# Weight sums made by adding transfers, and a second seven-product form in the first pair of groups two to four of an MLP

## The chip, the cores and the metric

The kernel runs on one core of a Trainium2 chip. The metric is device time in microseconds (us) of one execution, the median of several runs. The engines are named as in the profile: PE (TensorE, matmuls) with PEld (its weight loads), DVE (VectorE), ACT (ScalarE), POOL (GpSimd) and SP (SyncE, which here only issues DMAs).

## What is computed

One decoder block on 256 tokens and 16 prepended meta tokens, with a model width of 2048, in float32:

```python
h = h + hybrid_mixer(rmsnorm(h, norm_mix_g[l]), ...)
h = h + squared_relu_mlp(rmsnorm(h, norm_mlp_g[l]), w_ff1[l], w_ff2[l])
return rmsnorm(h, final_norm_g)[:, N_META:]

def squared_relu_mlp(xn, w1, w2):
    return jnp.square(jax.nn.relu(xn @ w1)) @ w2
```

The mixer (forgetting attention beside gated linear attention) ends in two gates, two projections and an output projection w_out. The MLP has 8192 hidden columns; the mixer's outputs for the meta tokens aren't needed after it, so that the MLP works on 256 tokens.

## The kernel before

**Numbers.** Every float32 operand is split into a high part (a rounded copy, made by ACT) and a low part (the rest, subtracted by DVE), and a product of two operands is three matmuls: high x high, high x low, low x high. `cut` (L969) makes the split of a fetched tile of weights into a buffer `w`, of which there are five. The fetched tile itself, `raw`, has five buffers too.

**Pairs.** The MLP runs in four groups of 2048 hidden columns. In a group, the first MLP product (x2 times w_ff1, into `a`) takes two pairs, and the second (`a` times w_ff2) takes two more (in the last group one, whose columns 1024 on are done in another way by the tail). A pair (`pair_of`, L999) makes 1024 output columns, as two blocks f of 512, for 256 tokens, as two halves t of 128. Its contraction over 2048 rows goes in 16 row tiles of 128. The columns stage of the mixer, which makes the gates of 12 of the 16 column blocks, has three pairs of the same kind.

**Forms.** Two row tiles, both halves of the tokens and both blocks of columns make a plain step (`plain`): one fetched tile of weights (512 KB, 2 row tiles x 512 columns) per block, one split, and two products, one for each half of the tokens. A product (`product_into`, L987) is 2 x 3 = 6 matmuls of 128x512. Four row tiles at a time can instead be taken in a seven-product form: the operands are 2 x 2 blocks (two halves of the tokens by two pairs of row tiles; two pairs of row tiles by two blocks of columns), and 7 products (m1 to m7) of sums of blocks stand for 8. The sums of token blocks (`token_sums`, four of them, made by DVE and split) are kept in `s_x2` and `s_a`; the sums of weight blocks r11, r12, r21, r22 are made by DVE (`less`, L976, a subtraction of 128x1024) in held tiles hb, hc, hd, he (he is the tile sums4, which the profile calls sums). `pair_of` is given one or two token sums and then takes four or eight row tiles in one or two forms. Before, the second pair of the second MLP product in groups one to three, and the three pairs of the columns stage, have two forms; all others have one.

**What each step of a form does before.** `held` fetches r12 to b and r22 to c. `m1` fetches r11, multiplies it, and subtracts it from b. `m5` splits that difference and makes two more sums (with two forms) or one. `m6` and `m7` multiply the sums, `m3` multiplies r22 (fetched once more where there are two forms), `m2` fetches r21 and makes the last sum, and `m4` multiplies that. `m1` to `m7` add into four PSUM banks x, y, z, v, with two copies and two additions between them.

**Order.** The forms of the next pair are put between the plain steps of the present one: after plain step i run the form's steps n for which `at[n] == i` (a table of numbers in the main loop of the MLP, another in `columns`). A scheduler then sets each engine's order by priority. In the output projection before the MLP (a loop over 16 blocks j), the first pair's form is put after j = 3, 5, 8 and 11. Weight fetches are issued by SP, in order, as far ahead as there are free buffers; the reloads of s_x2 from its copy in DRAM (`kept_sums`, four quarters, at the start of the fourth pair's plain steps) are issued by POOL (L1378).

## Time and profile before

| | us |
|---|---|
| median of 3 runs | 1497.2 (1497.01 to 1497.43) |
| the profiled execution | 1497.08 |
| its span, first to last instruction | 1495.1 |
| PE busy | 1484.9 |
| DVE busy | 1193.2 |
| ACT busy | 878.4 |
| POOL busy | 119.8 |

The page divides the span into 40 equal slices and gives for each the busy share of an engine in tenths (9 is 90% or more), the clock that PE was granted and the busy share of the DMA engines. The chain that ended last is followed back from the last instruction, at each step to what released it. A row of a group of instructions has the line, engine and operation, what it writes and reads, shapes, the count, then busy us and mean ns of one, and then the idle time of the engine just before them and what ended it. In the kernel, DMAs moved 335.00 MB. The columns stage lies about at 480 to 690 us, the output projection at 755 to 840, the MLP at 840 to 1460.

### The profile page before, as it was taken

What the parts mean: (1) busy time and instruction counts of PE and PEld (TensorE: products, weight loads), DVE (VectorE), ACT (ScalarE), POOL (GpSimd) and SP (SyncE); (2) the same over time, 40 slices, a digit from 0 to 9 for tenths busy, and PEclk for the clock granted to TensorE, in tenths of its full rate; (3) what the DMA queues carried; (4) which work ended last, traced back from release to release, by engine and by line L of the source; (5) the groups of instructions that cost most, each with busy time, mean ns of one, the idle gap of its engine ahead of it and who ended that gap; (6) DMA issues with size and microseconds to landing.
All of it is one profiled execution on the core that took longest, in us unless ns stands there. A gap on an engine that the chain in (4) does not pass through costs nothing.

```text
span 1495.1 us, 22541 instructions
## 1 busy us (share of the span) xinstructions
PE 1484.9 (99%) x8374; PEld 1322.2 (88%) x8374; DVE 1193.2 (80%) x1578; ACT 878.4 (59%) x1246; POOL 119.8 (8%) x202
## 2 busy tenths in 40 slices
PE   9999999999999999999999999999999999999997
PEld 8999999999999888888988888888888888888887
DVE  7899858586677877876788889877998889898766
ACT  7765444455555555555566666666665566556645
POOL 6012100111111000000011100000000000000004
PEclk9999999999999999999999999999999999999999
DMA  9545555465547677678678678877777778888783
GB/s 325 176 145 185 182 170 180 159 213 170 169 163 247 212 224 233 205 230 286 223 248 253 204 248 264 267 230 242 250 244 249 230 250 252 266 260 273 249 277 110
DMA packets 242545, 335.00 MB, mean 224 GB/s; under 512 B 13130, under 2 KB 209748, under 8 KB 242180
## 3 DMA queue, kind: packets, MB, share of 16 engines
q1 hardware_dynamic: 219940, 299.22, 61.2%
q10 hardware_dynamic: 21360, 30.09, 6.5%
q0 software_dynamic: 1136, 4.27, 0.9%
q8 instruction: 65, 1.06, 0.3%
q14 instruction: 44, 0.36, 0.1%
HBM read 316.22 MB, written 17.31 MB: 223 GB/s over the span
## 4 chain that ended last, share of the span: by engine, by line
PE 96%; DVE 2%; issue 1%; ACT 1%; POOL 0%; POOLq 0%; DVEq 0%; ACTq 0%
PE bx L993 17%; PE ps L169 14%; PE bv L993 11%; PE by L993 11%; PE bz L993 11%; PE ps L170 7%; PE psa L174 5%; PE psa L178 5%; PE psa L176 4%; PE gla L993 4%; PE fox L993 2%; PE ps L429 1%; PE ps L431 1%; PE ps L1424 1%; DVE w L135 1%
## 5 line engine op out<-in xcount | busy, mean ns | idle before, releaser
L973 DVE TENSOR_TENSOR w<-raw,w 128x1024 fp32r<-128x1024 f32 x300 | 365.4, 1224 | 100.9 <-ACT w L972 96.6
L972 ACT CAST w<-raw 128x1024 fp32r<-128x1024 f32 x300 | 312.3, 1048 | 203.6 <-PE bx L993 68.2
L135 DVE TENSOR_TENSOR w<-raw,w 128x1024 fp32r<-128x1024 f32 x198 | 243.0, 1229 | 81.5 <-ACT w L134 80.1
L134 ACT CAST w<-raw 128x1024 fp32r<-128x1024 f32 x198 | 207.4, 1049 | 92.4 <-PE psa L178 30.3
L169 PE MATMUL ps<-x,w 128*128 128x512 f32 x543 | 184.4, 383 | 0.0
L174 PE MATMUL psa<-x,w 128*128 128x272 f32 x640 | 181.7, 285 | 0.0
L178 PE MATMUL psa<-x,w 128*128 128x272 f32 x640 | 179.6, 282 | 0.0
L176 PE MATMUL psa<-x,w 128*128 128x272 f32 x624 | 175.9, 282 | 0.0
L170 PE MATMUL ps<-x,w 128*128 128x256 f32 x543 | 149.0, 274 | 0.0
L993 PE MATMUL bx<-w,x 128*128 128x512 f32 x528 | 131.1, 381 | 0.0
L174 PEld LDWEIGHTS psa<-x,w 128*128 128x128 f32 x640 | 120.2, 188 | 0.2
L178 PEld LDWEIGHTS psa<-x,w 128*128 128x128 f32 x640 | 120.2, 188 | 0.1
L176 PEld LDWEIGHTS psa<-x,w 128*128 128x128 f32 x624 | 117.4, 188 | 0.0
L169 PEld LDWEIGHTS ps<-x,w 128*128 128x128 f32 x543 | 101.9, 188 | 17.1
L993 PEld LDWEIGHTS bx<-w,x 128*128 128x128 f32 x528 | 98.8, 188 | 17.4
L993 PE MATMUL by<-w,x 128*128 128x512 f32 x444 | 112.5, 381 | 0.0
L170 PEld LDWEIGHTS ps<-x,w 128*128 128x128 f32 x543 | 102.0, 188 | 0.0
L993 PEld LDWEIGHTS by<-w,x 128*128 128x128 f32 x444 | 83.2, 188 | 14.6
L993 PE MATMUL bv<-w,x 128*128 128x512 f32 x360 | 91.9, 381 | 0.0
L993 PE MATMUL bz<-w,x 128*128 128x512 f32 x360 | 91.6, 381 | 0.0
L169 PE MATMUL ps<-y,w 128*128 128x512 f32 x256 | 85.6, 380 | 0.0
L993 PE MATMUL bx<-w,a 128*128 128x512 f32 x336 | 83.7, 380 | 0.0
(405 smaller groups left out, 2741.1 us busy)
## 6 DMA issues: line engine op xcount, KB each, us to landing
raw<-w_all_dram SPq DMA_DIRECT2D x489, 512.0 KB, 4.6
there<-turn ACTq DMA_DIRECT2D x80, 128.0 KB, 3.9
turn<-there ACTq DMA_DIRECT2D x20, 512.0 KB, 4.7
hb<-w_all_dram SPq DMA_DIRECT2D x18, 512.0 KB, 4.4
hc<-w_all_dram SPq DMA_DIRECT2D x18, 512.0 KB, 5.3
raw<-w_all_dram SPq DMA_DIRECT2D x26, 256.0 KB, 5.0
raw<-w_all_dram SPq DMA_DIRECT2D x8, 384.0 KB, 6.8
hd<-w_all_dram SPq DMA_DIRECT2D x6, 512.0 KB, 7.1
```

The source lines that it names most:

```text
L134: copied = nc.scalar.copy(hi[:, k, :], r).ins
L135: return copied, nc.vector.tensor_tensor(lo[:, k, :], r, hi[:, k, :].bitcast(F32), op=ALU.subtract).ins
L169: nc.tensor.matmul(steps(ps), hi, steps(row(x)), start=first, stop=False)
L170: nc.tensor.matmul(steps(ps[:, 0:NT]), lo, steps(x[:, 0, :]), start=False, stop=last)
L174: nc.tensor.matmul(steps(ps[:, X_LO]), hi, steps(x_lo[:, k]), start=first, stop=False, skip_group_check=True)
L176: nc.tensor.matmul(steps(ps[:, 0:NA]), lo, steps(x_hi[:, k]), start=False, stop=last and hi is None, skip_group_check=True)
L178: nc.tensor.matmul(steps(ps[:, 0:NA]), hi, steps(x_hi[:, k]), start=False, stop=last, skip_group_check=True)
L429: nc.tensor.matmul(steps(ps), hi, steps(row(x[:, k])), start=st, stop=False)
L431: nc.tensor.matmul(steps(ps[:, 0:NT]), lo, steps(x[:, k, 0]), start=False, stop=sp)
L972: copied = nc.scalar.copy(hi, r).ins
L973: made(copied, nc.vector.tensor_tensor(lo, r, hi.bitcast(F32), op=ALU.subtract).ins, 1)
L993: nc.tensor.matmul(steps(ps), l, steps(r), start=start and k == 0 and i == 0, stop=False, skip_group_check=True)
```

## The change

A transfer issued by POOL adds r22, as it comes from DRAM, onto a held tile (`gain_block`, a DMA with an accumulating add): onto b after m1 has used it, and, with two forms, onto a after m5's split. The signs of the sums change with that, in `token_sums` too. r22 isn't fetched to a held tile of its own any more where there are two forms, and `less` is left with m1 and m2 (and m5, as an addition, with one form). a is now always a held tile, not the fetched r11.

With the tiles so freed, the first pair of the first MLP product in groups two to four takes two forms, with the sums of x2's first eight row tiles in s_x2 and s_a. The second sums are made in the output projection from blocks 4 to 7 (at j = 9), stored to DRAM at j = 13, and reloaded with the first in groups two to four. The tables of places change: in `columns` for the first pair, and in the MLP for the pairs with two forms and for those beside a shorter rest.

```diff
@@ token_sums
-        nc.vector.tensor_tensor(c, src(0, 1), src(1, 1), op=ALU.add)
-        nc.vector.tensor_tensor(s3, src(0, 0), src(0, 1), op=ALU.subtract)
-        nc.vector.tensor_tensor(d, c, src(0, 0), op=ALU.subtract)
+        nc.vector.tensor_tensor(c, src(0, 1), src(1, 1), op=ALU.subtract)
+        nc.vector.tensor_tensor(s3, src(0, 1), src(0, 0), op=ALU.subtract)
+        nc.vector.tensor_tensor(d, src(0, 0), c, op=ALU.subtract)
@@ columns
+    def gain_block(raw, c0, k0):
+        nc.gpsimd.dma_start(raw.rearrange("p (c k m) -> p c k m", k=2, m=P),
+                            w_all[c0 : c0 + 4, :, k0 * P : (k0 + 2) * P].rearrange("c p (k m) -> p c k m", m=P),
+                            accum_op=ALU.add)
@@ pair_of
         def held(q):
-            got["b", q], got["c", q] = fetched(f2, 4 * q, ("hb", "hd")[q]), fetched(f2, 4 * q + 2, ("hc", "he")[q])
+            got["b", q] = fetched(f2, 4 * q, ("hb", "hc")[q])
+            if nq == 1:
+                got["c", q] = fetched(f2, 4 * q + 2, "hc")
 
         def m1(q):
             r11 = fetched(f1, 4 * q)
             w = split_of(r11)
-            got["a", q] = r11 if nq > 1 else holder("hd")
+            got["a", q] = holder(("hd", "he")[q])
             less(got["a", q], got["b", q], r11)
+            gain_block(got["b", q], f2, 4 * q + 2)
             product("x", own(0, 4 * q), w, q == 0)
...
         def m5(q):
             w = split_of(got["a", q])
             if nq > 1:
-                less(got["b", q], got["c", q], got["b", q])
-                less(got["c", q], got["c", q], got["a", q])
+                gain_block(got["a", q], f2, 4 * q + 2)
             else:
-                less(got["a", q], got["c", q], got["a", q])
+                less(got["a", q], got["c", q], got["a", q], ALU.add)
             product("v", summed(q, 0), w, q == 0)
...
         def m6(q):
-            w = split_of(got["c" if nq > 1 else "a", q])
-            if nq == 1:
-                less(got["b", q], got["c", q], got["b", q])
+            w = split_of(got["a", q])
             product("x", summed(q, 1), w)
@@ pairs
-                yield (g, p), lambda: pair_of(blocks(), x2, [s_x2], lambda f, pt, g=g, p=p: hidden(
+                yield (g, p), lambda: pair_of(blocks(), x2, [s_x2, s_a] if p == 0 and g in TWO else [s_x2], lambda f, pt, g=g, p=p: hidden(
@@ output projection
-        if j < 4:
-            nc.vector.tensor_scalar(gained[:, NT * j : NT * (j + 1)], ht[:, j, :], gain(1, j), None, op0=ALU.mult)
-        if j == 3:
+        if j == 4:
+            gained = turn_tile()
+        if j < 8:
+            nc.vector.tensor_scalar(gained[:, NT * (j % 4) : NT * (j % 4 + 1)], ht[:, j, :], gain(1, j), None, op0=ALU.mult)
+        if j in (3, 9):
...
-            token_sums(s_x2, lambda i, t: g4[:, 2 * i : 2 * i + 2, t], gained[:, 4 * NT :])
+            token_sums(s_x2 if j == 3 else s_a, lambda i, t: g4[:, 2 * i : 2 * i + 2, t], gained[:, 4 * NT :])
...
-        if j == 8:
-            nc.scalar.dma_start(kept_sums, s_x2.bitcast(F32))
+        if j in (8, 13):
+            nc.scalar.dma_start(kept_sums[j // 13], (s_x2 if j == 8 else s_a).bitcast(F32))
@@ main loop of the MLP
-              3: (0, 2, 4, 5, 5, 6, 6, 7)}.get(index % 4, (0, 2, 3, 4, 5, 7, 9, 10))
+              3: (0, 1, 1, 3, 2, 3, 4, 4, 5, 5, 5, 6, 6, 6, 7, 7) if len(steps_next) > 8 else (0, 2, 4, 5, 5, 6, 6, 7),
...
-                    nc.gpsimd.dma_start(s_x2[:, q].bitcast(F32), kept_sums[:, q])
+                    for tile_of, kept_of in list(zip((s_x2, s_a), kept_sums))[0 : len(steps_next) // 8]:
+                        nc.gpsimd.dma_start(tile_of[:, q].bitcast(F32), kept_of[:, q])
```

How this moves instructions is shown at the first pair of group two, whose form or forms stand between the plain steps of the pair before it (the second pair of group one's second product). First PE, before: by, bx, bz, bv with the operand a are plain products, those with x2 or s_x2 belong to the form (m1 with w_1348, m5 with w_1356, m6 with w_1361).

```order
L993 MATMUL by_1307_9622<-w_1346_9912,a_1220_8986 128x4x32x4 x6
L993 MATMUL bx_1295_9529<-w_1346_9912,a_1220_8986 128x4x32x4 x6
L993 MATMUL bx_1350_9934<-w_1348_9929,x2_1064_7876 128x4x32x4 x6
L993 MATMUL by_1307_9622<-w_1353_9945,a_1220_8986 128x4x32x4 x6
L993 MATMUL bx_1295_9529<-w_1353_9945,a_1220_8986 128x4x32x4 x6
L993 MATMUL bz_1316_9690<-w_1355_9964,a_1220_8986 128x4x32x4 x6
L993 MATMUL bv_1300_9565<-w_1355_9964,a_1220_8986 128x4x32x4 x6
L993 MATMUL bv_1357_9983<-w_1356_9979,s_x2_7880 128x4x32x4 x6
L993 MATMUL bz_1316_9690<-w_1360_9994,a_1220_8986 128x4x32x4 x6
L993 MATMUL bv_1300_9565<-w_1360_9994,a_1220_8986 128x4x32x4 x6
L993 MATMUL bx_1350_9934<-w_1361_10009,s_x2_7880 128x4x32x4 x6
```

The same place on PE now, from the second form's m1 (w_1353) on; m5 has w_1357 and w_1359, m6 has w_1363 and w_1364.

```order
L999 MATMUL bx_1349_9927<-w_1353_9953,x2_1064_7870 128x4x32x4 x6
L999 MATMUL by_1306_9611<-w_1356_9968,a_1221_8993 128x4x32x4 x6
L999 MATMUL bx_1297_9538<-w_1356_9968,a_1221_8993 128x4x32x4 x6
L999 MATMUL bz_1319_9712<-w_1362_10010,a_1221_8993 128x4x32x4
L999 MATMUL bv_1301_9570<-w_1362_10010,a_1221_8993 128x4x32x4
L999 MATMUL bv_1358_9989<-w_1357_9985,s_x2_7874 128x4x32x4 x6
L999 MATMUL bv_1358_9989<-w_1359_9996,s_a_7875 128x4x32x4 x6
L999 MATMUL bz_1319_9712<-w_1362_10010,a_1221_8993 128x4x32x4 x5
L999 MATMUL bv_1301_9570<-w_1362_10010,a_1221_8993 128x4x32x4 x5
L999 MATMUL bx_1349_9927<-w_1363_10025,s_x2_7874 128x4x32x4 x6
L999 MATMUL bx_1349_9927<-w_1364_10034,s_a_7875 128x4x32x4
```

Between the start of m5 and that of m6 there stood 18 matmuls before; now there are 22, m5 of the second form among them.

DVE at the same place, before, from the split of m1's weights (w_1348) to that of m6's (w_1361): three subtractions (L977) make the sums, two of them behind m5's split.

```order
L973 TENSOR_TENSOR w_1348_9929<-raw_1347_9927,w_1348_9929 128x1024
L977 TENSOR_TENSOR hd_1349_9932<-hb_1341_9889,raw_1347_9927 128x1024
L973 TENSOR_TENSOR w_1353_9945<-raw_1352_9943,w_1353_9945 128x1024
L973 TENSOR_TENSOR w_1355_9964<-raw_1354_9962,w_1355_9964 128x1024
L973 TENSOR_TENSOR w_1356_9979<-hd_1349_9932,w_1356_9979 128x1024
L977 TENSOR_TENSOR hd_1349_9932<-hc_1342_9891,hd_1349_9932 128x1024
L973 TENSOR_TENSOR w_1360_9994<-raw_1359_9992,w_1360_9994 128x1024
L973 TENSOR_TENSOR w_1361_10009<-hd_1349_9932,w_1361_10009 128x1024
L977 TENSOR_TENSOR hb_1341_9889<-hc_1342_9891,hb_1341_9889 128x1024
```

DVE there now, from the last plain split ahead of the forms (w_1344) to that of the second m6 (w_1364). ACT's copies of the same tiles stand in the same order.

```order
L974 TENSOR_TENSOR w_1344_9902<-raw_1343_9900,w_1344_9902 128x1024
L974 TENSOR_TENSOR w_1347_9921<-raw_1346_9919,w_1347_9921 128x1024
L978 TENSOR_TENSOR hd_1348_9924<-hb_1342_9898,raw_1346_9919 128x1024
L974 TENSOR_TENSOR w_1351_9936<-raw_1350_9934,w_1351_9936 128x1024
L974 TENSOR_TENSOR w_1353_9953<-raw_1352_9951,w_1353_9953 128x1024
L978 TENSOR_TENSOR sums4_78<-hc_1345_9917,raw_1352_9951 128x1024
L974 TENSOR_TENSOR w_1356_9968<-raw_1355_9966,w_1356_9968 128x1024
L974 TENSOR_TENSOR w_1357_9985<-hd_1348_9924,w_1357_9985 128x1024
L974 TENSOR_TENSOR w_1359_9996<-sums4_78,w_1359_9996 128x1024
L974 TENSOR_TENSOR w_1362_10010<-raw_1361_10008,w_1362_10010 128x1024
L974 TENSOR_TENSOR w_1363_10025<-hd_1348_9924,w_1363_10025 128x1024
L974 TENSOR_TENSOR w_1364_10034<-sums4_78,w_1364_10034 128x1024
```

The subtractions between m5's and m6's splits are gone; in their place, hd and sums4 are added to by POOL's transfers, which no row of DVE shows. With five buffers, w_1357 takes the one of w_1344 (w_1347, w_1351, w_1353 and w_1356 lie between), and w_1359 that of w_1347.

POOL before had, between the sums of squares of the output projection and those of the tail, nothing but the reloads.

```order
L1207 TENSOR_TENSOR acc2_7885<-acc2_7885,hsq_1178_8702 128x256
L1207 TENSOR_TENSOR acc2_7885<-acc2_7885,hsq_1185_8754 128x256
L1207 TENSOR_TENSOR acc2_7885<-acc2_7885,hsq_1192_8806 128x256
L1378 DMA s_x2_7880<-kept_sums_7884 128x512 x12
L1207 TENSOR_TENSOR acc3_8813<-acc3_8813,hsq_1859_13611 128x256
```

POOL now, from the second form of the pair before (sums4_78) to the four additions of the first pair of group two (hb and hc after m1, hd and sums4 after m5):

```order
L981 DMA sums4_78<-w_all_dram 128x4x256
L1389 DMA s_x2_7874<-kept_sums_7878 128x512
L1389 DMA s_a_7875<-kept_sums2_7879 128x512
L1389 DMA s_x2_7874<-kept_sums_7878 128x512
L1389 DMA s_a_7875<-kept_sums2_7879 128x512
L1389 DMA s_x2_7874<-kept_sums_7878 128x512
L1389 DMA s_a_7875<-kept_sums2_7879 128x512
L981 DMA hb_1342_9898<-w_all_dram 128x4x256
L1389 DMA s_x2_7874<-kept_sums_7878 128x512
L981 DMA hc_1345_9917<-w_all_dram 128x4x256
L981 DMA hd_1348_9924<-w_all_dram 128x4x256
L981 DMA sums4_78<-w_all_dram 128x4x256
```

The reloads now alternate between s_x2 and s_a, and the additions stand among them in one queue: hc, hd and sums4 follow the last reload, with nothing between them.

More of the change, by code (lines that the diff above doesn't have):

```diff
@@ L1078, in m4 @@
         def m4(q):
-            product("x", own(1, 4 * q + 2), split_of(got["c" if nq > 1 else "a", q]))
+            product("x", own(1, 4 * q + 2), split_of(got["a", q]))
         if nq == 1:
```

15 lines of the change are left out of this document (9 added, 6 removed).

## The prediction, before the changed kernel ran

> **What bounds the kernel now.** I read the page first, then the waits of TensorE (PE), then the busy time by stretches, then the timeline at the place that the change makes tighter, and last the DMA issues. The page gives the span, the busy time, the 40 slices and the chain that ended last:
>
> ```profile
> span 1495.1 us, 22541 instructions
> PE 1484.9 (99%) x8374; PEld 1322.2 (88%) x8374; DVE 1193.2 (80%) x1578; ACT 878.4 (59%) x1246; POOL 119.8 (8%) x202
> PE   9999999999999999999999999999999999999997
> DVE  7899858586677877876788889877998889898766
> PEclk9999999999999999999999999999999999999999
> DMA  9545555465547677678678678877777778888783
> PE 96%; DVE 2%; issue 1%; ACT 1%; POOL 0%; POOLq 0%; DVEq 0%; ACTq 0%
> ```
>
> PE is busy in every slice at full clock and makes 96% of the chain. PE's own waits, longest first (us in total, times, longest), come to two us over the whole span:
>
> ```profile
> PE warm L393 <- DVE ones L274: 1.3, 1, 1.3
> PE pr L287 <- DVE csl L255: 0.3, 1, 0.3
> ```
>
> So a matmul that goes shortens the run by its own spacing, and nothing that DVE, ACT or DMA saves is worth anything, unless PE starts to wait. The price of a matmul is in the stretch of the MLP where only products run (us, then busy time and count of each engine, PE clock, DMA share, GB/s); the other rows are used below:
>
> ```profile
> 776.00:812.00 36.00, 36.00 (x210) 32.26 (x209) 33.24 (x41) 24.23 (x37) 6.35 (x6) 1.00 0.77 248
> 855.00:1425.00 570.00, 570.00 (x2593) 486.36 (x2592) 486.50 (x491) 360.33 (x413) 6.52 (x12) 1.00 0.79 251
> 1320.00:1340.00 20.00, 20.00 (x93) 17.06 (x92) 18.32 (x20) 11.00 (x12) 0.00 (x0) 1.00 1.01 325
> ```
>
> 570.00 / 2593 = 0.220 us for one 128x512 matmul. (A matmul's own 0.38 us overlaps its neighbours and is not its price.)
>
> **Part 1, fewer products.** A pair has 16 row tiles. With one seven-product form (four row tiles) it takes 7 products and 12 plain row tiles of 2 products each, 31 in all. With two forms it takes 14 and 8 x 2 = 16, so 30. Groups two to four have one such pair each: 3 products, of 6 matmuls each, 18 matmuls x 0.220 = 3.96 us. The built programs agree: 3744 matmuls of that line before, 3726 now. This is all on the path. It also excludes that the change doesn't do what it says.
>
> **Part 2, DVE and ACT.** One subtraction of 128x1024, one split on each engine, and the small steps of the sums cost:
>
> ```profile
> L973 DVE TENSOR_TENSOR w<-raw,w 128x1024 fp32r<-128x1024 f32 x300 | 365.4, 1224 | 100.9 <-ACT w L972 96.6 <-DMA turn<-there 1.2
> L972 ACT CAST w<-raw 128x1024 fp32r<-128x1024 f32 x300 | 312.3, 1048 | 203.6 <-PE bx L993 68.2 <-PE bv L993 61.6 <-issue 13.2
> L977 DVE TENSOR_TENSOR hb<-hc,hb 128x1024 f32<-128x1024 f32 x18 | 22.5, 1248 | 0.0
> L1267 DVE TENSOR_SCALAR turn<-h 128x256 f32<-128x256 f32 x4 | 2.8, 709 | 0.0
> L909 DVE TENSOR_TENSOR turn<-turn 128x256 f32<-128x256 f32 x1 | 0.4, 425 | 0.0
> L255 DVE TENSOR_TENSOR s_x<-turn,s_x 128x1024 fp32r<-128x1024 f32 x1 | 1.2, 1218 | 0.0
> ```
>
> Weight sums on DVE: before, 24 forms x 4 = 96; now 18 forms in two-form pairs x 2 and 9 alone x 3 = 63. That is 33 x 1.22 = 40 us less. Splits: a second form takes 7 where 4 plain row tiles took 4, so 9 more, 9 x 1.22 = 11 us on DVE and 9 x 1.05 = 9.4 us on ACT. None of it is on the path, so I cost both signs at nothing. The cover is the lead of the weights over PE, and it is thinnest in the output projection, where the second sums of x2 come in: 4 x 0.71 + 4 x 0.42 + 1.22 = 5.7 us more on DVE between j = 4 and 10, less 1.25 for the sum into hb that a transfer now makes. In the stretch 776 to 812 DVE has 33.24 of 36 us; with 4.5 more it is 1.7 us over. The lead must absorb that; below I say what if not.
>
> **Part 3, the transfers.** SP issues 12 fetches fewer (a form's own stay at four, and the three new second forms replace four plain fetches each), POOL issues 45 adding transfers of 512 KB (18 x 2 + 9), and 24 reloads of 256 KB instead of 12; ACT stores a second 1 MB of sums once. That is 33 x 0.524 + 12 x 0.262 + 1.05 = 21.5 MB on top of 335.0, spread over stretches where the DMA engines stand at 0.79. Each adding transfer must also read the 512 KB that it adds to. I cost this at nothing except in one stage.
>
> **Part 4, the new wait.** An adding transfer makes ACT's split wait for a landing where it used to wait for a DVE subtraction. Behind that split in ACT's queue stand all later splits and the copies out of PSUM; behind a transfer in POOL's queue stand the reloads of the sums and the next transfers; SP's fetch into hb waits for the split of m7, as before. How far apart are the product that starts the transfer (m5: its split releases a) and the product that needs it (m6)? By the new order of PE at 0.220 us per matmul, start to start: 7.9 to 14.5 us in the column pairs, 10.6 and 11.9 us in the second pair of the second product. But in the first pair of groups two to four m5 starts at 8.36 us after the last product of w_1344 and m6 at 13.20: 38 and 60 matmuls later, 4.84 us apart. For m7 it is 14 us or more. So only this place is tight, three times.
>
> The time allowed is that distance, plus the lead with which m5's split is done before PE uses it, less one split on ACT and DVE. The same place in before, m5 and m6 of group two's first pair, shows the lead:
>
> ```profile
> 979.40 1.23 DVE L973 TENSOR_TENSOR w<-hd,w 128x1024 fp32r<-128x1024 f32 x1 [1.30 <-ACT w L972]
> 987.32 1.48 PE L993 MATMUL bv<-w,s_x 128*128 128x512 f32 x6
> 983.80 1.22 DVE L973 TENSOR_TENSOR w<-hd,w 128x1024 fp32r<-128x1024 f32 x1 [0.53 <-ACT w L972]
> 991.28 1.48 PE L993 MATMUL bx<-w,s_x 128*128 128x512 f32 x6
> 942.50 1.23 DVE L973 TENSOR_TENSOR w<-sums,w 128x1024 fp32r<-128x1024 f32 x1
> 945.52 0.38 PE L993 MATMUL bx<-w,s_x 128*128 128x512 f32 x1
> ```
>
> The first two pairs of rows give 987.32 - 980.63 = 6.7 us and 991.28 - 985.02 = 6.3 us. The last pair, 40 us earlier, where DVE also has four subtractions, gives 1.8 us. In the new order five weight buffers set the lead: w_1357 (m5) takes that of w_1344, free at 0; 1.05 + 1.22 = 2.3 us later it is split, 6.1 us ahead of PE. I take 6.1, since DVE has only 22 splits and 4 subtractions (32 us) in this stage's 30 x 6 x 0.220 = 39.6 us. Allowed: 4.84 + 6.1 - 2.3 = 8.6 us, and for the second form 8.6 too, since both its products stand one product later.
>
> What does an adding transfer take? No row shows one. The nearest rows (KB each, median us from issue to landing):
>
> ```profile
> raw<-w_all_dram SPq DMA_DIRECT2D x489, 512.0 KB, 4.6
> there<-turn ACTq DMA_DIRECT2D x80, 128.0 KB, 3.9
> turn<-there ACTq DMA_DIRECT2D x20, 512.0 KB, 4.7
> hd<-w_all_dram SPq DMA_DIRECT2D x6, 512.0 KB, 7.1
> s_x<-kept_sums POOLq DMA_DIRECT2D x12, 256.0 KB, 4.6
> 944.22 0.60 POOL L1378 DMA_DIRECT2D s_x<-kept_sums  x1 [100.36 <-PE bv L993]
> ```
>
> The lower end is a plain fetch, 4.6 us. The upper end is the slowest plain kind and once more what it moves beyond a small one: 7.1 + (7.1 - 3.9) = 10.3 us, or 12 if two wait for each other on the queue. I take the row of POOL's own queue, 4.6 us for 256 KB, plus a half of 4.7 - 3.9 for the larger size (0.4), plus one reading of 512 KB at the 325 GB/s above (1.6) for the second operand: 6.6 us. The second form's transfer is issued a split later and shares the queue, some 8 us. Both land inside 8.6 us, with little to spare; I put 0.15 us per group, 0.5 us in all, on it.
>
> The Trainium skill, "DMA: Bandwidth & Descriptors", section "Anatomy of one DMA — SWDGE (gpsimd) path", fits such a transfer by about 2.0 us plus bytes at 436 GB/s, which is 2.6 us for the 256 KB reload. The trace disagrees: its row says 4.6. By that fit an adding transfer would take 3.2 us, PE would never wait, and the run would be 1497.08 - 3.96 = 1493.1 us.
>
> **The sum.** The profiled execution took 1497.08 us, 1.98 more than its span and 0.12 less than the median of 1497.2. 1497.08 - 3.96 + 0.5 = 1493.6; on the median, 1493.7, which is 0.23% faster. About 0.2% (3.0 us) is what a measurement of this kernel can tell from no change.
>
> **Rivals.** *The transfer lands late (slower side).* ACT then waits for a, and PE runs out of weights at m6 in the three first pairs. Every us beyond 8.6 costs 3 us. At 9.9 us the saving is gone, from 10.9 us on it is slower by over 0.2%; at 12 us, 3 x 3.4 - 3.96 = 6.2 us slower, 1503.4. For it: three transfers within four us on one queue. Against it: the lead of 6.3 to 6.7 us above. Chance 0.27, of which 0.16 within 0.2% and 0.11 slower.
>
> *The DMA engines become the bound in that stage.* In 39.6 us there are 20 tiles and 8 reloads, 20 x 0.524 + 8 x 0.262 = 12.6 MB, 318 GB/s, against 325 in the row with share 1.01. With the second readings 14.7 MB, 45 us at 325: 5.6 us late per group, up to 16.8 in all, from which the five fetch buffers (8 us of transfers) take most if they were full. Half of it gives 8.4 - 4.0 = 4.4 us slower, 1501.5. It decides as soon as PE waits on raw rather than on a. The Trainium skill, "Collectives: The Full Stack", section "The bandwidth ceiling: the fold count and why AG ≠ RS ≠ AR", says that an add in a DMA reads two sources on one ring and so runs at half the rate of a copy. No run here shows that yet; by it the 14.7 MB count in full. Chance 0.15, 0.04 within and 0.11 slower.
>
> *DVE is late in the output projection.* 1.7 us of overrun and no lead to absorb it: 1495.3, within 0.2%. Against it, PE never waited there. Chance 0.08.
>
> *More than the count.* In the columns a matmul stands 0.2215 us apart, not 0.220:
>
> ```profile
> 480.00:690.00 210.00, 210.00 (x948) 176.61 (x947) 161.29 (x151) 114.74 (x122) 0.73 (x1) 1.00 0.71 228
> ```
>
> If that came from DVE's traffic, which falls there, 948 x 0.0017 = 1.6 us more would go: 1492. Chance 0.04.
>
> **Chances and range.** The forecast has 0.46. Faster: 0.46 + 0.04 = 0.50; within 0.2%: 0.16 + 0.04 + 0.08 = 0.28; slower: 0.11 + 0.11 = 0.22. The range goes from 1491.5 (the last rival) to 1503.5 (the first at 12 us); what is left out is the upper part of the second rival and of still later landings, under 2 in 10. The likeliest case alone is 1493.1 to 1494.3.
>
> **What would show it.** Right: 3726 product matmuls with PE idle under 1 us in the fourth stage of each group; adding transfers land in 6 to 8.5 us; DVE busy about 23 us less. Wrong: waits of PE or ACT at m6's weights that end with a landing of a (first rival), or waits of ACT on raw with a DMA share of 1.0 (second); a wait of PE in the output projection (third).

## The result and the profile after

The changed kernel takes 1539.5 us (median of 3 runs, 1538.18 to 1544.33) against 1497.2 before: the ratio is 1.0289, with a 95% interval of 1.0274 to 1.0303. It is slower by 42 us, far outside the forecast range. The profiled execution took 1538.18 us, its span is 1536.4.

The page of the changed kernel, in the lines that answer to those shown of before:

```profile
span 1536.4 us, 22681 instructions
PE 1504.0 (98%) x8356; PEld 1320.3 (86%) x8356; DVE 1166.8 (76%) x1563; ACT 880.3 (57%) x1256; POOL 185.6 (12%) x259
PE   9999999999999999999999999999999999999997
PEclk9999999999999999999999999999999999999999
DMA  9545545464468788887687889978998889999883
q1 hardware_dynamic: 213604, 292.93, 58.4%
q0 software_dynamic: 25856, 31.01, 11.3%
PE 17%; DMA 5%; DVE 3%; issue 3%; ACT 2%; POOL 0%; ACTq 0%; POOLq 0%; DVEq 0%
PE bx L999 5%; DMA sums<-w_all_dram 4%; PE by L999 3%; PE bz L999 3%; PE bv L999 3%; DVE w L974 2%; ACT w L973 1%; DMA there<-turn 1%; PE ps L170 1%; PE ps L1435 1%; PE ps L1417 0%; PE ps L171 0%; DMA hb<-w_all_dram 0%; DVE hd L978 0%; DVE sums L978 0%
```

The row of PE's digits still reads 9 in nearly every slice: a slice is 38 us long, and a stall of 3 us in it doesn't show. What shows is that a transfer, `sums<-w_all_dram`, stands second on the chain, where before PE had 96% of it. (The shares of this chain add up to 30% of the span: it couldn't be followed back further.) PE's busy time also grew by 19.1 us with 18 matmuls fewer, which is the first sign that the matmuls themselves became slower; by the sums below, 11.9 us come from that, and the rest isn't broken down here.

The waits of the changed kernel (us in total, times, longest):

```profile
ACT w L973 <- DMA hd<-w_all_dram: 38.5, 6, 9.2
ACT w L973 <- DMA sums<-w_all_dram: 28.3, 6, 7.4
ACT w L973 <- DMA he<-w_all_dram: 17.1, 3, 7.1
PE bx L999 <- ACT w L973: 12.7, 9, 2.8
PE bx L999 <- DVE w L974: 4.3, 6, 0.8
ACT w L973 <- DMA raw<-w_all_dram: 0.3, 1, 0.3
```

ACT's splits wait for adding transfers (hd, sums, he), and hardly at all for plain fetches (raw). PE then waits for ACT. The three waits for he lie in the columns stage (at 502, 572 and 643 us), where PE didn't stand: ACT's lead took them. Two places in the MLP show how PE comes to stand. POOL's issues, ACT's splits and PE's products in the second pair of the second product, group two's end (start, us, engine, line, what; in brackets idle time before and its releaser):

```profile
1099.66 1.27 POOL L981 DMA_DIRECT2D hb<-w_all_dram  x1 [32.00 <-ACT turn L1324]
1104.08 1.27 POOL L981 DMA_DIRECT2D hd<-w_all_dram  x1 [3.15 <-DVE w L974]
1107.49 1.27 POOL L981 DMA_DIRECT2D hc<-w_all_dram  x1 [2.13 <-DVE sums L978]
1108.72 0.63 POOL L1389 DMA_DIRECT2D s_a<-kept_sums  x1
1110.31 1.27 POOL L981 DMA_DIRECT2D sums<-w_all_dram  x1 [0.96 <-DVE w L974]
1115.30 1.05 ACT L973 CAST w<-hd 128x1024 fp32r<-128x1024 f32 x1 [5.75 <-DMA hd<-w_all_dram]
1126.64 1.04 ACT L973 CAST w<-sums 128x1024 fp32r<-128x1024 f32 x1 [7.42 <-DMA sums<-w_all_dram]
1127.74 0.49 PE L999 MATMUL bx<-w,s_x 128*128 128x512 f32 x1 [2.81 <-ACT w L973]
1129.00 2.50 PE L999 MATMUL bx<-w,s_x 128*128 128x512 f32 x5 [0.78 <-DVE w L974]
```

Four adding transfers and a reload are issued within 12 us; I call that a bunch. The tile hd is used 11.2 us after the issue of its transfer, and sums, the last, 16.3 us after. ACT has nothing to split for 7.42 us, its lead over PE is gone, and PE stands 2.81 us and once more 0.78 us. The five matmuls behind take 2.50 us where five take 1.26 at full clock. ACT's splits in the first pair of the first product, 48 us later (the place that the prediction called tight):

```profile
1175.51 1.04 ACT L973 CAST w<-hd 128x1024 fp32r<-128x1024 f32 x1 [9.15 <-DMA hd<-w_all_dram]
1179.00 1.04 ACT L973 CAST w<-sums 128x1024 fp32r<-128x1024 f32 x1 [2.45 <-DMA sums<-w_all_dram]
```

The issue of that hd was at 1163.06, 12.4 us before, and that of sums at 1164.40, 14.6 us before. There are six such places: the second pair of the second product in groups one to three, and the first pair of the first product in groups two to four, in turn. With the matmuls at half clock right behind them they lost 3.9, 6.4, 7.4, 7.4, 6.2 and 4.2 us, in order of time.

The DMA issues (count, KB, median us from issue to landing) give the size of what the prediction had put at 6.6 and 8 us:

```profile
raw<-w_all_dram SPq DMA_DIRECT2D x489, 512.0 KB, 4.9
hb<-w_all_dram POOLq DMA_DIRECT2D x18, 512.0 KB, 8.3
hd<-w_all_dram POOLq DMA_DIRECT2D x9, 512.0 KB, 11.1
hc<-w_all_dram POOLq DMA_DIRECT2D x9, 512.0 KB, 10.6
sums<-w_all_dram POOLq DMA_DIRECT2D x6, 512.0 KB, 14.7
```

**Where the 42 us are.** From the first product of the MLP to its last, before took 602.15 us and after 642.35, which is 40.2 of the difference. I took the distance between each two neighbouring matmuls of the product line in the trace and set it against 220.0 ns: distances under 260 ns give what I call pace; those up to 460 ns while the PE clock stands at 0.5, half clock; all others, stalls. The windows over 20 us in two of the places (busy us and count of PE, PEld, DVE, ACT, POOL, then PE clock, DMA share, GB/s):

```profile
1100.00:1120.00 20.00, 20.00 (x93) 17.07 (x92) 14.16 (x15) 10.17 (x12) 5.97 (x7) 1.00 1.11 259
1120.00:1140.00 20.00, 16.30 (x59) 12.39 (x58) 12.22 (x13) 9.67 (x11) 2.11 (x4) 0.83 0.97 299
1140.00:1160.00 20.00, 20.00 (x91) 16.77 (x90) 18.57 (x20) 10.78 (x11) 2.43 (x4) 1.00 0.92 278
1300.00:1320.00 20.00, 16.26 (x64) 12.20 (x63) 14.81 (x15) 10.93 (x12) 2.15 (x4) 0.91 0.95 296
```

Three things are to be seen. While a bunch of adding transfers runs (1100 to 1120), the DMA engines stand at a share of 1.11 and move only 259 GB/s; before, in the stretch 1320 to 1340, a share of 1.01 went with 325. (The share is the sum of the packets' times over 16 engines; above 1, packets overlap.) The plain fetches beside the bunch are late too: of the five that SP issued between 1100 and 1111 us, the four whose landing the trace has landed after 9.0 to 17.5 us, against the median of 4.9 in the list above. So it isn't POOL's queue alone that is slow. Behind a stall the clock falls: 0.83 in the second row is 0.5 over 6.8 us. And behind that, at full clock and with no wait, 91 matmuls fit into 20 us and not 93: the distance is 223.4 ns on the mean and not 220.0, up to the next stall. The sum over the MLP: -3.96 (18 matmuls) + 32.25 (stalls) + 4.59 (half clock) + 7.31 (pace) = 40.19 us.

### The profile page after: what moved, and what is told of

It reads as the page before. It is cut to its first block, busy times and chain, and to the rows that moved or that the text cites. A ratio compares the mean times of both kernels' runs of the same rounds, so it can differ in the third digit from the quotient of the medians.

```text
span 1536.4 us, 22681 instructions
## 1 busy us (share of the span) xinstructions
PE 1504.0 (98%) x8356; PEld 1320.3 (86%) x8356; DVE 1166.8 (76%) x1563; ACT 880.3 (57%) x1256; POOL 185.6 (12%) x259
## 2 busy tenths in 40 slices
DMA packets 261074, 356.51 MB, mean 232 GB/s; under 512 B 13866, under 2 KB 227380, under 8 KB 260580
## 3 DMA queue, kind: packets, MB, share of 16 engines
q1 hardware_dynamic: 213604, 292.93, 58.4%
q0 software_dynamic: 25856, 31.01, 11.3%
## 5 line engine op out<-in xcount | busy, mean ns | idle before, releaser
L974 DVE TENSOR_TENSOR w<-raw,w 128x1024 fp32r<-128x1024 f32 x288 | 349.1, 1224 | 73.2 <-ACT w L973 68.8
L973 ACT CAST w<-raw 128x1024 fp32r<-128x1024 f32 x288 | 297.4, 1047 | 131.0 <-PE bx L999 37.8
L136 DVE TENSOR_TENSOR w<-raw,w 128x1024 fp32r<-128x1024 f32 x198 | 244.2, 1234 | 81.2 <-ACT w L135 79.9
L135 ACT CAST w<-raw 128x1024 fp32r<-128x1024 f32 x198 | 207.6, 1049 | 93.2 <-PE psa L179 30.3
L999 PE MATMUL bx<-w,x 128*128 128x512 f32 x528 | 134.6, 383 | 0.0
L973 ACT CAST w<-hd 128x1024 fp32r<-128x1024 f32 x54 | 56.5, 1047 | 104.9 <-DVE hd L978 47.5
L974 DVE TENSOR_TENSOR w<-hd,w 128x1024 fp32r<-128x1024 f32 x54 | 65.9, 1221 | 62.2 <-ACT w L973 62.0
L999 PEld LDWEIGHTS by<-w,x 128*128 128x128 f32 x426 | 79.8, 187 | 15.1
L999 PE MATMUL bx<-w,a 128*128 128x512 f32 x336 | 86.8, 384 | 0.0
L999 PE MATMUL bz<-w,x 128*128 128x512 f32 x324 | 86.1, 384 | 0.6 <-DVE w L974 0.5
## 6 DMA issues: line engine op xcount, KB each, us to landing
hd<-w_all_dram POOLq DMA_DIRECT2D x9, 512.0 KB, 11.1
```

The costliest lines, as they stand in the source:

```text
L135: copied = nc.scalar.copy(hi[:, k, :], r).ins
L136: return copied, nc.vector.tensor_tensor(lo[:, k, :], r, hi[:, k, :].bitcast(F32), op=ALU.subtract).ins
L973: copied = nc.scalar.copy(hi, r).ins
L974: made(copied, nc.vector.tensor_tensor(lo, r, hi.bitcast(F32), op=ALU.subtract).ins, 1)
L999: nc.tensor.matmul(steps(ps), l, steps(r), start=start and k == 0 and i == 0, stop=False, skip_group_check=True)
```

## The experiments

Theory 1 is the one that the waits suggest: an adding transfer takes longer than m5 and m6 are apart, so m6 waits. Theory 2: the DMA engines are full, since the added bytes and the second readings are more than they can move. Theory 3: the second forms by themselves cost, by their order of products. The table gives all kernels by the same sums over the MLP (us; matmuls are those saved x 0.220):

| kernel | median us | ratio (95%) | matmuls | stalls | half clock | pace |
|---|---|---|---|---|---|---|
| before | 1497.2 | | | 0.00 | 0 | 0.00 |
| after | 1539.5 | 1.0289 (1.0274 to 1.0303) | -3.96 | 32.25 | 4.59 | 7.31 |
| sums by DVE | 1500.9 | 1.0021 (1.0012 to 1.0030) | -3.96 | 1.86 | 0 | 4.33 |
| a's sum by DVE | 1505.18 | 1.0053 (1.0040 to 1.0067) | -3.96 | 6.81 | 0 | 4.82 |
| later m6 | 1538.81 | 1.0276 (1.0257 to 1.0295) | -3.96 | 33.60 | 4.03 | 5.26 |
| one form again | 1511.51 | 1.0094 (1.0075 to 1.0112) | 0 | 7.74 | 0 | 4.00 |
| transfers that don't add | 1501.29 | 1.0026 (1.0016 to 1.0037) | -3.96 | 3.32 | 0 | 3.67 |
| before, three splits held up | 1508.37 | 1.0071 (1.0052 to 1.0089) | 0 | 2.64 | 0 | 2.80 |
| sums by DVE, mended | 1499.44 | 1.0013 (1.0004 to 1.0022) | -3.96 | 2.29 | 0 | 1.74 |
| and b in m6 | 1500.88 | 1.0025 (1.0016 to 1.0034) | -3.96 | 1.95 | 0 | 3.94 |
| and turns by POOL | 1498.36 | 1.0008 (0.9999 to 1.0016) | -3.96 | 3.09 | 0 | 3.45 |
| and two groups only | 1500.4 | 1.0013 (0.9998 to 1.0029) | -2.64 | 0.00 | 0 | 5.71 |
| mended, two groups only | 1494.75 | 0.9977 (0.9968 to 0.9985) | -2.64 | 0.00 | 0 | 0.00 |

The columns of stalls, half clock and pace are of the one profiled execution, the median is over all runs. For each kernel these terms give the length of its MLP to 0.02 us.

### Sums by DVE

```diff
@@ m1
-            gain_block(got["b", q], f2, 4 * q + 2)
@@ m5
-            if nq > 1:
-                gain_block(got["a", q], f2, 4 * q + 2)
-            else:
-                less(got["a", q], got["c", q], got["a", q], ALU.add)
+            r22 = fetched(f2, 4 * q + 2) if nq > 1 else got["c", q]
+            less(got["a", q], r22, got["a", q], ALU.add)
+            less(got["b", q], r22, got["b", q], ALU.add)
```

> The second forms in two row-tile pairs stay (3726 matmuls on the forms' lines, as in the changed kernel), but no transfer adds: SyncE fetches r22 plainly and VectorE adds it to a and to b right behind m5's split. Theory 1 (the adding transfer lands 8 to 15 us after its issue, m6's split waits for it, TensorE stands): the waits of TensorE on the splits fall back to about 2 us, the MLP has no half-clock stretch, and the time is 1493 to 1496 us, the kernel before less 18 matmuls. Theory 2 (the DMA engines are the bound, since there are 21.5 MB more): r22 is still fetched a second time, so some 16 MB of the extra bytes stay, raw tiles come late, and the time stays over 1505 us. Theory 3 (the second forms themselves cost, by their order of products and their VectorE work): 1515 us or more.

1500.9 us. Theory 3 is out: the same forms, without adding transfers, lose 38.6 us less. The waits on adding transfers are gone (ACT still waits 12.5 us for raw), and 1.86 us of stalls are left. But 1493 to 1496 was missed: the pace takes 4.33 us, more than the 3.96 that were saved. The windows of this kernel, before and behind a stall of 0.6 us at 1081:

```profile
960.00:980.00 20.00, 20.00 (x93) 17.06 (x92) 15.95 (x15) 12.51 (x15) 0.54 (x1) 1.00 0.88 295
1100.00:1120.00 20.00, 20.00 (x91) 16.80 (x90) 17.59 (x17) 12.24 (x14) 2.15 (x4) 1.00 0.99 328
```

Here no half clock comes in, so the slower pace doesn't need it. In this trace the mean distance is 220.0 ns from 851 us up to the stall at 1081, 223.4 behind it, 220.0 behind the next one (0.1 us, at 1245), and 223.4 behind the last (1.0 us, at 1323).

### Only a's sum by DVE

```diff
@@ m5
-            if nq > 1:
-                gain_block(got["a", q], f2, 4 * q + 2)
-            else:
-                less(got["a", q], got["c", q], got["a", q], ALU.add)
+            r22 = fetched(f2, 4 * q + 2) if nq > 1 else got["c", q]
+            less(got["a", q], r22, got["a", q], ALU.add)
```

> Only the sum that m5 makes for m6 (a + r22) goes from the adding transfer to VectorE with a plain fetch; the sum for m7 (b + r22) is still added by a transfer. Theory 1: m6 no longer waits for a transfer, m7's transfer has 15 us or more of lead, so 1493 to 1498 us. Theory 2: the same bytes as in the changed kernel, half of the adding transfers: over 1510 us. Theory 3: no gain against the changed kernel, 1530 us or more.

1505.18 us: 34 of the 42 us go with the a transfers alone, and theory 2 in its plain form (so many bytes) is out, since this kernel moves 356.52 MB, as the changed one does (356.51). But theory 1 missed too, by 7 us. Theory 1 says that b's transfers have all the lead they need; the waits of this kernel say otherwise:

```profile
ACT w L973 <- DMA raw<-w_all_dram: 25.8, 11, 4.6
ACT w L973 <- DMA hb<-w_all_dram: 9.6, 3, 3.7
```

The row of hb is the wait of m7's split for b's own adding transfer, issued by POOL some 10 us before. The row of raw is waits for plain fetches. The sums by DVE, which have no adding transfer at all, wait 12.5 us for raw, so about half of the 25.8 us can be put down to b's transfers.

### Later m6

```diff
-        at = {1: (0, 3, 4, 5, 6, 8, 9, 10), 2: (0, 1, 1, 2, 3, 4, 5, 7, 7, 8, 8, 8, 9, 9, 10, 11),
-              3: (0, 1, 1, 3, 2, 3, 4, 4, 5, 5, 5, 6, 6, 6, 7, 7) if len(steps_next) > 8 else (0, 2, 4, 5, 5, 6, 6, 7),
+        at = {1: (0, 3, 4, 5, 6, 8, 9, 10), 2: (0, 1, 1, 2, 2, 3, 7, 7, 7, 8, 8, 8, 9, 9, 10, 11),
+              3: (0, 1, 1, 2, 2, 2, 5, 5, 6, 6, 6, 6, 7, 7, 7, 7) if len(steps_next) > 8 else (0, 2, 4, 5, 5, 6, 6, 7),
```

> All transfers and products of the changed kernel stay; only the slots of the steps change, so that between the last m5 and the m6 that needs its sum lie about 12 to 13 us of products where 4.8 (first product) and 10.6 (second product) lay. Theory 1: most of the stall goes, 36 us of waits on the two places become 5 to 15, and the time is 1500 to 1515 us. Theory 2: the bytes per us are the same, the wait only moves to other steps, 1535 us or so. Theory 3: the same forms, 1535 us or so.

1538.81 us, no gain. Theory 1 as a matter of distance falls. The waits of this kernel:

```profile
ACT w L973 <- DMA sums<-w_all_dram: 43.3, 6, 8.0
ACT w L973 <- DMA he<-w_all_dram: 17.2, 3, 7.1
ACT w L973 <- DMA raw<-w_all_dram: 15.2, 7, 5.1
ACT w L973 <- DMA hb<-w_all_dram: 14.1, 5, 6.0
ACT w L973 <- DMA hd<-w_all_dram: 3.8, 3, 1.9
```

The wait for hd fell from 38.5 to 3.8 us, as more distance should make it. But the steps ahead of m6 moved together, so the four transfers of a bunch are issued closer to each other, and the waits for sums and for raw grew by 15.0 and 14.9 us. So what is short in the bunch seems to be not time between two steps but room on the DMA engines: the windows of this kernel over two bunches stand above a share of 1.0 at a low rate:

```profile
920.00:940.00 20.00, 20.00 (x93) 17.06 (x92) 15.36 (x16) 12.50 (x16) 6.27 (x6) 1.00 1.06 248
1100.00:1120.00 20.00, 20.00 (x91) 16.79 (x90) 11.34 (x10) 7.86 (x9) 4.98 (x5) 1.00 1.14 254
```

### One form again in the first product

```diff
-TWO = (1, 2, 3)
+TWO = ()
```

> Adding transfers everywhere as in the changed kernel, but the first pair of the first product in groups two to four goes back to one second form of four row tiles (3744 matmuls). Theory 1: the three waits in the first product's pairs go, the three in the second product's second pair (3.9, 7.4 and 6.2 us, with the slower matmuls behind them) stay: 1515 to 1522 us. Theory 2: 9 adding transfers less of 18, some 8 MB less: between 1510 and 1525 us, with waits on raw tiles. Theory 3: all of the loss goes, 1497 us.

1511.51 us. The three places in the first product go, the three in the second stay, as theory 1 had it, but they cost 7.74 us and not 17.5. Beside them POOL has 12 reloads rather than 24, which may be the reason; no run separates that. ACT's waits for raw are 0.2 us, so theory 2 was wrong on who would wait.

### Transfers that don't add

```diff
-                            w_all[c0 : c0 + 4, :, k0 * P : (k0 + 2) * P].rearrange("c p (k m) -> p c k m", m=P),
-                            accum_op=ALU.add)
+                            w_all[c0 : c0 + 4, :, k0 * P : (k0 + 2) * P].rearrange("c p (k m) -> p c k m", m=P))
```

> The changed kernel with the same transfers at the same places of POOL's queue, of the same size, but plain: they overwrite the tile instead of adding to it, so the add of r22 is left out of a and of b. Theory 2, in the form that the late-m6 run leaves (an adding transfer costs the DMA engines about twice a plain one, and a bunch of three of them fills the engines for 20 us, so these and the raw tiles beside them land late): the sums land 5 to 8 us after their issue, the engines' share in the bunch falls under 1.0, and the time is 1494 to 1505 us. Theory 1, in the form that is left (POOL's queue takes one transfer after the other, 3 to 5 us each, whatever it does at the target): the sums still land 11 to 15 us after issue and the time is over 1525 us. Theory 3 (the second forms): 1525 us or more.

1501.29 us: 38 of the 42 us go with the add alone. (The kernel leaves the sums with r22 out, so it doesn't compute the block; it serves for the time.) The number of issues, their places and the 31.01 MB of the queue are the same. The DMA rows of this kernel, to be set beside those of after:

```profile
q0 software_dynamic: 8576, 31.01, 6.3%
hb<-w_all_dram POOLq DMA_DIRECT2D x18, 512.0 KB, 6.6
hd<-w_all_dram POOLq DMA_DIRECT2D x9, 512.0 KB, 6.9
sums<-w_all_dram POOLq DMA_DIRECT2D x6, 512.0 KB, 8.1
```

And its windows over the bunch that the changed kernel has at 1100 us (here its four transfers are issued from 1087.90 to 1098.96) and behind it:

```profile
1080.00:1100.00 20.00, 20.00 (x91) 16.77 (x90) 18.55 (x18) 15.12 (x19) 3.56 (x5) 1.00 0.94 313
1100.00:1120.00 20.00, 20.00 (x92) 17.08 (x91) 14.44 (x14) 12.39 (x15) 2.18 (x4) 1.00 0.93 313
```

The landings fall from 11.1 to 6.9 us (hd) and from 14.7 to 8.1 us (sums), near the 6.6 and 8 us that the prediction had estimated for transfers that do add. The same bytes load the engines by 6.3% of 1499.0 us, 94.4 us; with the add by 11.3% of 1536.4, 173.6 us. The difference over 45 adding transfers is 1.76 us of all 16 engines for each, on top of 94.4 / 31.01 x 0.524 = 1.60 us that 512 KB take without it: an adding transfer costs the engines 2.1 times a copy. One thing besides the add differs between the two kernels, the size of the packets: queue 0 has 25856 packets with the add and 8576 without, for the same bytes. It isn't the cause: SP's fetches (q1 in the page above) have packets of 1.4 KB on the mean, and their 58.4% of 1536.4 us for 292.93 MB makes 1.61 us per 512 KB, as much as POOL's larger packets without the add. Single packets say the same: one of 1 KB takes 101 ns (median) with the add in the changed kernel, and 46 ns in SP's fetches there.

The share of time alone doesn't tell the two kernels apart. From the issue of hd to the use of sums the engines are full in both: a share of 1.14 in the changed kernel (1104 to 1126 us), and 1.03 here (1092 to 1108). What differs is what they move in that time, 268 GB/s there and 356 here. The plain fetches beside the bunch are late without the add too, up to 13.4 us (those issued from 1080 to 1100 us). This shows the cause: theory 2 in the form that a bunch is too much for the engines because each add takes about as much engine time as a second copy, and not the total of the run.

The Trainium skill, "Collectives: The Full Stack", section "The bandwidth ceiling: the fold count and why AG ≠ RS ≠ AR", says of a collective that its add needs two source reads and that it so runs at half the rate of one that copies. The trace agrees in the size, with 2.1 times; it doesn't show the reads themselves. The fit of the Trainium skill for a transfer by POOL that the prediction cites ("DMA: Bandwidth & Descriptors", section "Anatomy of one DMA — SWDGE (gpsimd) path"; 3.2 us for 512 KB) doesn't hold here: 6.6 to 8.1 us without the add, 8.3 to 14.7 with it.

### Splits held up in the kernel before

The pace needed a test without adding transfers and without the new forms.

```diff
+    cuts = [0]
+
     def cut(raw, low=False):
@@
+        cuts[0] += not low
+        for _ in range({90: 6, 150: 7, 210: 8}.get(cuts[0], 0)):
+            nc.scalar.copy(hi, r)
         copied = nc.scalar.copy(hi, r).ins
```

> The kernel before with three splits of the MLP held up: ScalarE makes the high half 6, 7 and 8 times more before the copy that counts. Nothing else is changed. If a stall of TensorE by itself sets the pace of the matmuls behind it: the spacing in the MLP is 220.0 ns up to the first stall, then for stretches of a hundred matmuls and more 222.7 to 228.3 ns until another stall, and the time is above 1497 us by the stalls plus 2 to 6 us. If the slower pace of the changed kernel comes from its added transfers or its second forms: 220.0 ns behind every stall, and the time is above 1497 us by the stalls alone.

In this trace the pace changes only at stalls. The first and the third of the held-up splits made stalls (1015 to 1023 and 1265 to 1284 us); the second made none. The mean distance is 220.0 ns up to the first stall, 220.0 again from 1023 to 1265 us, over 1100 matmuls, and 223.33 over 729 behind the last. The stalls are 2.64 us, the pace 2.80, in the profiled execution of 1503.05 us, the fastest of its four runs (up to 1512.20); what the slower runs lost more isn't known. So a stall by itself is enough to set the pace anew, to the fast one or to a slower one. The windows of this kernel between the stalls and behind the last:

```profile
1100.00:1240.00 140.00, 140.00 (x638) 119.43 (x637) 118.66 (x119) 93.01 (x104) 2.15 (x4) 1.00 0.77 243
1290.00:1400.00 110.00, 110.00 (x494) 92.26 (x493) 96.20 (x101) 66.30 (x75) 0.54 (x1) 1.00 0.81 258
```

The second stretch in before:

```profile
1290.00:1400.00 110.00, 110.00 (x501) 93.86 (x501) 95.84 (x100) 66.32 (x75) 0.54 (x1) 1.00 0.83 262
```

Before has 501 matmuls there where this one has 494, with PE busy throughout in both.

### A version without adding transfers that keeps the saving

Five more kernels go after what is left in the sums by DVE: small stalls, each of which may set the slow pace. First the two that the trace names. At 1081 us a sum stood on DVE behind the token sums, which waited for ACT; at 1323 ACT stood at the issue of a reload behind the transfers of a turn.

```diff
-                behind.append([2, lambda: summed(back)])
+                behind.append([3, lambda: summed(back)])
@@ reload
-            nc.scalar.dma_start(ht[:, js, :], kept[:, 4 * b * NT : 4 * (b + 1) * NT].rearrange("p (j t) -> p j t", t=NT))
+            nc.gpsimd.dma_start(ht[:, js, :], kept[:, 4 * b * NT : 4 * (b + 1) * NT].rearrange("p (j t) -> p j t", t=NT))
```

> The run with sums by VectorE, with its two stalls mended: the token sums of a hidden block go one split later on VectorE, and the reload of the residual is issued by POOL and not by ScalarE. If the 18 saved matmuls were eaten by these stalls and the slower pace behind them: no stall over 0.3 us in the MLP behind 860 us, 220.0 ns throughout, 1492.5 to 1495 us. If VectorE's greater load is what costs: other stalls take their place, 1497 to 1501 us.

1499.44 us, in the range of the second expectation. The stall at 1081 is gone and the pace is fast up to 1319; behind it come stalls at 1319, 1353 and 1386, all in the last group, where DVE also adds the residual. Whether DVE's load makes them isn't shown. Next, b's sum:

```diff
@@ m5
-            less(got["b", q], r22, got["b", q], ALU.add)
+            got["r", q] = r22
@@ m6
+            less(got["b", q], got["r", q], got["b", q], ALU.add)
```

> As the mended run with sums by VectorE, and the add of r22 to b goes from m5, where it stands on VectorE ahead of a split that TensorE needs first, to m6. If the two stalls of 0.4 us at m5 (851 and 1386 us) came from that order: they go, the one-time stalls at 1319 and 1353 us (ScalarE held by its turn transfers) stay, the pace is 220.0 ns up to 1319 us, and the time is 1494 to 1498 us. If not: 1497 to 1501 us as before this edit.

1500.88 us. The first expectation failed: at 851 us there had been no stall at all (PE has other matmuls between the products there), the one at 1386 came back as two at 1388 and 1391 us, those at 1319 and 1353, which were to stay, are gone, and from a new one of 0.15 us at 1064 on the pace is slow. Nothing follows on the order, except that it isn't the only cause in the last group. Then the turns, on top of that (`by` is the engine that issues; POOL for the hidden blocks but the last, and for the last two gathered ones):

```diff
-                nc.scalar.dma_start(there.rearrange("(i s) (c e) -> c s i e", i=4, c=4)[c],
+                by.dma_start(there.rearrange("(i s) (c e) -> c s i e", i=4, c=4)[c],
@@
-            behind.append([slots[1], lambda: nc.scalar.dma_start(back, there)])
+            behind.append([slots[1], lambda: by.dma_start(back, there)])
```

> As the run with b's add in m6, and the turn transfers of the MLP are issued by POOL, which has nothing else to do there, not by ScalarE. If ScalarE's waits on those transfers made the stalls at 1319 and 1353 us: no stall is left behind 860 us, 220.0 ns throughout, and the saved matmuls show: 1492.5 to 1495 us, under the kernel before. If POOL's issues land later and VectorE waits for them in turn: stalls behind the turns, 1497 us or more.

1498.36 us, the second expectation: there are stalls in the last group, of 3.09 us in all. Last, both versions with two forms in groups two and three alone:

```diff
-TWO = (1, 2, 3)
+TWO = (1, 2)
```

> As the run with the turn transfers issued by POOL, but the last group's first pair goes back to one second form (3732 matmuls, 12 under the kernel before): there VectorE also adds the residual, and all stalls that are left lay in that group. If those stalls are all that eats the saving: no stall behind 860 us, 220.0 ns throughout, 1494 to 1496 us, 2.6 us under the kernel before less what is left at 840 us. If stalls appear elsewhere: 1497 to 1499 us.

> The same two groups on the mended run with sums by VectorE, whose turn transfers ScalarE issues and whose b is added in m5. Stalls of 0.4 us at m5 and those behind ScalarE's turn transfers can stay: 1495 to 1498 us, and not under the run with POOL's turns by more than a microsecond.

The second of these is the version to keep: 1494.75 us (1494.30 to 1495.36) against 1497.92 for before beside it, 0.9977 (0.9968 to 0.9985). My expectation had the order of the two the wrong way round, and 1500.4 us of the first lies outside both of its ranges. The window of the version to keep:

```profile
855.00:1425.00 570.00, 570.00 (x2592) 486.36 (x2592) 502.40 (x506) 365.15 (x420) 12.35 (x22) 1.00 0.82 260
```

And that of the other, which has no stall either:

```profile
855.00:1425.00 570.00, 570.00 (x2568) 481.15 (x2567) 497.58 (x502) 362.75 (x416) 59.16 (x107) 1.00 0.82 259
```

Both have PE busy throughout and the clock at 1.00, and still one fits 24 matmuls more into 570 us. In the slower trace the distances are 220 ns up to 1063 us, then 225, 221, 221, 230 and 241, and 223.33 on the mean from there to the end of the MLP. So a delay of some 40 ns over five matmuls stands where the pace changes; what made it isn't known. Its runs lie between 1495.0 and 1510.0 us, those of the other within 1.1 us. In the version to keep the MLP takes 599.51 us, and 602.15 - 12 x 0.220 = 599.51.

## Why the prediction was wrong

**Part 1, fewer products: right.** 3726 matmuls of the product line, and the price of 0.220 us holds where the pace does: the last version saves its 12 x 0.220 us to 0.01.

**Part 2, DVE and ACT: right.** DVE's busy time fell by 26.4 us (1193.2 to 1166.8; about 23 were expected), and it bought nothing. The output projection, from the last product of the columns to the first of the MLP, took 141.5 us in both (697.52 to 839.02 before, 698.47 to 839.94 after), so the rival with DVE late there was wrong.

**Part 3, the transfers: the bytes right (335.00 to 356.51 MB), the cost wrong.** The prediction read the DMA engines at 0.79 over the MLP as room and costed the transfers at nothing except in one stage. What counts is the stretch of 20 us in which a bunch is issued, and there the share is 1.0 to 1.1 at a rate of 200 to 260 GB/s.

**Part 4, the new wait: the step that failed.** "What does an adding transfer take?" was answered with 6.6 us, and some 8 for the second; it took 8.3 to 11.1, and 14.7 for the last of a bunch. The estimate was 5.0 us for the plain transfer and 1.6 for the second reading. The second term was near: 1.76 us of engine time, and 8.3 against 6.6 us for the landing in hb. The first was too small: without the add that landing takes 6.6 us, so that 6.6 us in both is chance. And the estimate has no term for the bunch: four such transfers and the plain fetches beside them share the same engines, so that each waits for the others' adds too. I put the step from 8.3 us (hb) to 11.1 (hd) and 14.7 (sums) down to that. The allowed time of 8.6 us was fair: at the place in group three, 12.4 us from issue to use of hd less 8.6 gives 3.8 us, 14.6 for sums less 8.6 gives 6.0, and PE's stalls there are 3.0 us for the first and 5.9 in all.

From the wrong landing came the second error: "only this place is tight, three times". The second pair of the second product, with 10.6 us between m5 and m6, counted as safe against 8 us; against the 16.3 us of sums it isn't. So there were six places and not three.

**The rivals.** The first (the transfer lands late) named the mechanism and one of the two places; at 12 us it gave 1503.4, since it priced three places, one stall each, and nothing behind a stall. The second (the DMA engines as the bound) named the cause of the lateness, but put the wait on the plain fetches, and in the MLP ACT's splits waited for the sums instead (0.3 us on raw against 66.8 on hd and sums). Its full figure of 5.6 us late per group, before it was halved, is near the stalls in the three first pairs, 6.4, 5.9 and 4.2 us; the other three places it didn't have. The two were one chain, and the prediction held them apart as alternatives. The last rival was wrong as well: the columns took 217.25 us against 216.78.

**What no part of it had.** A stall costs more than its length: 4.59 us at half clock and 7.31 us of pace in the changed kernel, 12 of the 42 us.

## What to carry to other kernels

A DMA that adds isn't a copy with an add for free: count it as two on the DMA engines, and look at the share and the rate over the 20 us in which it is issued, not over the stage. Moving the consumer later didn't help here, as the issues moved together with it; giving the add to an engine with spare time did. Spreading the issues would be the other way, and no run tried it. In a kernel where PE never waits, compare the count of matmuls in equal windows: a pace that is 1.5% off eats a saving of 18 matmuls. To remove the last small stalls brought it back in one version of two; in the other the pace slowed without one.

## What the hardware showed unexpectedly

- **The distance between matmuls has steps.** With PE busy and the granted clock at 1.00, the distance of neighbouring 128x512 matmuls of the MLP is 220.0, 222.7, 223.3 or 228.3 ns, as the mean of a stretch (at 223.3 most single distances are from 221 to 226), and it mostly stays for more than a hundred matmuls until the next stall. In the changed kernel it was 220.0 up to the first stall (951 us), 223.3 or 223.4 in four stretches between later ones, back at 220.0 in two (from 1093 and 1271 us), 228.3 or 228.4 in two (from 1313 and 1361 us), and 222.7 in the last (from 1396 us). The held-up splits show that a stall alone can do it, and that the next one can undo it; the first version with two groups shows that it can also change without a stall. What in PE sets the value, and why one stall changes it and another doesn't, stays open.
- **PE's clock after a stall.** Behind three stalls of 2.7 to 3.0 us of the changed kernel the record shows a clock of 0.5 for 6.8, 6.8 and 3.4 us. In the run with later m6 it does so behind stalls of 2.5 and 2.8 us, and not behind one of 2.7 us, so length alone doesn't decide.
- **POOL's issue of an adding transfer takes longer.** 1.27 us for 512 KB with the add, 0.75 without, by the timelines of the two kernels.

A row of each, of the changed kernel in the list above at 1099.66, and of the one whose transfers don't add:

```profile
1095.71 0.75 POOL L981 DMA_DIRECT2D hc<-w_all_dram  x1 [2.66 <-DMA there<-turn]
1098.96 0.76 POOL L981 DMA_DIRECT2D sums<-w_all_dram  x1 [1.47 <-issue]
```
